# Forming the low part of a split weight by an adding transfer instead of a VectorE subtraction, for 120 of 168 weight tiles

## The chip, the cores and the metric

The kernel runs on one core of a Trainium2 chip. The metric is device time in microseconds for one execution of the whole program. The engines are named as in the profile: PE (TensorE, with PEld for its weight loads), DVE (VectorE), ACT (ScalarE), POOL (GpSimd) and SP (SyncE, which here only issues transfers).

## The reference, cut to what matters

One inference step of a decoder trunk of two layers, in float32, for 512 prompt tokens and 32 sample tokens (8 sequences of 4), which share all weights. Model width 1024, FFN width 2816, 16 query heads and 4 key heads of 64, window 128, depthwise convolution of 31 taps. Each layer is an FFN, a mixing stage, and a second FFN, with a norm behind each:

```python
x = layer_norm(ALPHA * x + 0.5 * swiglu(x, ffn1_up, ffn1_down), ...)
proj = x @ w_in + b_in
q, k, v, glu, gates = jnp.split(proj, SPLITS, axis=-1)
u = u_a * jax.nn.sigmoid(u_g)
attn = window_attention(q, k, v, ...)          # ALiBi and sinks
c = silu(layer_norm(causal_depthwise(u, ...), ...))
mix = sigmoid(g_attn) * (attn @ w_attn_out) + sigmoid(g_conv) * (c @ w_conv_out)
x = layer_norm(ALPHA * x + mix @ w_out, ...)
x = layer_norm(ALPHA * x + 0.5 * swiglu(x, ffn2_up, ffn2_down), ...)
```

## The kernel before, in words

**Products in three passes.** A float32 operand is split into a high part, rounded to the format `F32R` that PE multiplies, and a low part, the rest. A product is three matmuls: high weight by high activation (line 432), high weight by low activation (433), low weight by high activation (434). `unit` (419) does this for one piece of weights (up to 8 blocks of 128 rows, 256 columns) and one half of the tokens (`hf`): 8 x 2 x 3 = 48 matmuls, the low part being needed at the third. The tokens, 544, lie along the free dimension and are cut at 272. The values (1103) use the same three passes in lines 1115 to 1117.

**Pieces.** `plan` lists all weight pieces in the order of their use. `fetch` (254) issues a piece's loads on SP, as two tiles `raw` of 128 x 1024 from a pool of 5 buffers. `prep` (281) then calls `halves` (272) for each tile: ACT copies it into `wh`, rounding (277), DVE subtracts `wh` from it into `wl` (278). `wh` and `wl` come from the pool `pair` with 37 buffers, which also holds activations. This way goes every piece of the mixing stage, and the first four pieces of each FFN (two of the gate half, `a`, and two of the other, `u`); 84 pieces, 168 tiles. All other FFN weights go another way, `steps` (293), planned piece by piece with costs written out by hand, and aren't touched.

**When a piece is prepared.** `W` (410) prepares pieces until two are ahead of the one asked for (four at the start of an FFN); `ahead` (405) prepares the next stage's first pieces during the last products of an FFN, with ACT's copy pinned to its place in the program (`keep_in_program_order`). Apart from such pins, the order of each engine's instructions is laid out when the program is built, by a scheduler that takes what is ready first in its own timing, and of that the earliest in the program. Each engine, POOL with its transfers included, then executes its list strictly in order.

**The mixing stage** (`mix`, 984) takes its pieces in the order k, ug0, ua0, v, q0, q1, ug1, ua1, q2, q3, ug2, ua2, ug3, ua3, ga0, ga1, ao0, ga2, ao1, ga3, ao2, ao3, then four each of gc, co and wo. `ug` and `ua` make the gated input of the convolution; behind each of the four `ua` comes a part of the convolution, whose 30 taps per channel block run on DVE (1075) as background work, spread over the attention by `pump`. The sample tokens' part of the convolution is products on POOL (1090, 16 for each part), sums on DVE (1093) and bias additions on POOL (1094). `ga` is the attention's gate (`gate`, 1337), `ao` the attention's output product, `gc` and `co` the same for the convolution, `wo` the output. POOL also issues all small output transfers: values (1123, 1127), keys (1138, 1141), convolution state (1400, 1402).

**Norms.** `ln_fin` (451) has three steps, put off into the next products by a clock of PE's work: `centre` (a matmul for the mean at 463, DVE subtractions 468, ACT squares 472, DVE sums 474 and 481), `newton` (a matmul at 485, then a chain of some 14 tiny DVE operations, 507 to 521) and `scale` (a matmul at 493, DVE multiplications 497, then ACT's gain and bias, 530 or 1426, and the new split, 441 on ACT and 442 on DVE). The next stage's products of that half of the tokens need this split.

Of the kernel before, what the change touches and what calls it, by code (L numbers as in the profile page):

```python
# [11 lines left out]
F32 = mybir.dt.float32  # L12
F32R = mybir.dt.float32r
# [3 lines left out]
ALU = mybir.AluOpType  # L17
# [82 lines left out]
class Ker:  # L100
# [168 lines left out]
            raw.append(t)  # L269
        return key, kk, raw  # L270

    def halves(self, t, shape, small=False):

        new = lambda n: (self.f1(shape, F32R) if small else
                         self.pp.tile(shape, F32R, tag="pair", name=self.nm(n)))
        wh, wl = new("wh"), new("wl")
        ins = self.nc.scalar.copy(wh, t)  # L277
        self.nc.vector.tensor_tensor(wl, t, wh.bitcast(F32), op=ALU.subtract)  # L278
        return (wh, wl), ins

    def prep(self, pin=False, got=None):
        key, kk, raw = got or self.fetch()
        assert kk
        ms = []
        for t in raw:
            m, ins = self.halves(t, list(t.shape))
            if pin:
                self.tc.keep_in_program_order(ins)
            ms.append(m)
        self.ready.append((key, ms, kk))  # L290


# [1211 lines left out]
```

## Time and profile before

| | |
|---|---|
| Median of 3 runs | 2600.75 us (2594.13 to 2605.29) |
| Profiled execution | 2602.92 us, span 2600.8 us |
| Mean granted PE clock | 0.978 |
| ACT's share of the span | 46% |
| DVE's share of the span | 72% |
| DMA queues | 28.1% of 16 engines for SP's, 1.0% for POOL's |

A group's row in the profile gives the line, the engine, what is written from what, the shape and the count, then busy time and mean duration, then how long the engine idled before it and who ended that. Waits are given as total, number of times and longest. In a table of stretches, each row has the stretch, its length, busy time and count for each engine, the granted PE clock, the share of the DMA engines and GB/s. A row of a timeline is start, duration, engine, line, operation, tiles and count, with the idle time before it in brackets. Line 278 has one row with 168 instructions, since `halves` is a helper; places in the program are told by time.

### The profile page before, as it was taken

How to read it: one execution, taken by the hardware profiler on the slowest of the kernel's cores; microseconds unless marked ns; L12 is line 12 of the kernel's file. 1: busy time of each engine (PE TensorE's matmuls, PEld its weight loads, DVE VectorE, ACT ScalarE, POOL GpSimd, SP SyncE). 2: the span in 40 equal slices, each digit the busy share in tenths (PEclk: the TensorE clock that was granted, in tenths of full speed). 3: DMA queues.
4: the chain of work that ended last, by engine and by line, in shares of the span. 5: the costliest groups of instructions: out<-in, count | busy, mean ns of one | idle time of the engine just before them, and what ended most of it. 6: DMA issues, size and time to landing. Idle time of an engine off the chain costs nothing.

```text
span 2600.8 us, 47137 instructions
## 1 busy us (share of the span) xinstructions
PE 2522.6 (97%) x19846; PEld 2471.7 (95%) x19846; DVE 1882.3 (72%) x2955; ACT 1195.6 (46%) x2116; POOL 238.7 (9%) x323
## 2 busy tenths in 40 slices
PE   8999998999999999999999999999999999999997
PEld 8999998988999999999999999999899999999997
DVE  5776665997986577666667666669979766776665
ACT  4444434577426254444354444346873353444441
POOL 2000000722300000000100000026141000000000
PEclk9999998999999999999999999999999999999998
DMA  5333332231322223332503333322223222233321
GB/s 191 90 98 91 97 111 72 61 96 52 93 85 79 82 66 106 93 94 87 189 17 106 90 93 91 114 66 75 70 62 110 66 82 79 76 106 98 98 84 57
DMA packets 327139, 232.12 MB, mean 89 GB/s; under 512 B 43748, under 2 KB 324532, under 8 KB 326832
## 3 DMA queue, kind: packets, MB, share of 16 engines
q1 hardware_dynamic: 323088, 220.36, 28.1%
q0 software_dynamic: 3840, 8.76, 1.0%
q8 instruction: 155, 2.54, 0.4%
q14 instruction: 56, 0.46, 0.1%
HBM read 225.69 MB, written 9.16 MB: 90 GB/s over the span
## 4 chain that ended last, share of the span: by engine, by line
PE 84%; DVE 8%; ACT 4%; POOL 2%; issue 1%; DMA 0%; DVEq 0%; ACTq 0%; POOLq 0%
PE pa L646 17%; PE pa L434 17%; PE pa L432 17%; PE pa L433 17%; PE pb L646 12%; DVE pr L1075 3%; POOL f L1090 2%; DVE wl L278 1%; PE pa L1186 1%; PE pb L1215 1%; PE pb L1227 1%; DVE pr L442 1%; DVE pr L497 1%; PE pb L493 0%; ACT pr L1426 0%
## 5 line engine op out<-in xcount | busy, mean ns | idle before, releaser
L432 PE MATMUL pa<-pr,wh 128*128 128x272 f32 x2624 | 770.0, 295 | 24.0 <-ACT pr L441 18.5
L434 PE MATMUL pa<-pr,wl 128*128 128x272 f32 x2624 | 768.9, 294 | 6.2 <-DVE wl L278 6.2
L433 PE MATMUL pa<-pr,wh 128*128 128x272 f32 x2624 | 766.5, 293 | 5.8 <-DVE pr L442 5.8
L432 PEld LDWEIGHTS pa<-pr,wh 128*128 128x128 f32 x2624 | 502.2, 192 | 31.5 <-ACT pr L441 21.7
L433 PEld LDWEIGHTS pa<-pr,wh 128*128 128x128 f32 x2624 | 506.0, 193 | 10.6 <-DVE pr L442 8.2
L434 PEld LDWEIGHTS pa<-pr,wl 128*128 128x128 f32 x2624 | 502.8, 192 | 7.2 <-DVE wl L278 7.0
L432 PE MATMUL pa<-pr,wd 128*128 128x272 f32 (+2 forms) x1408 | 406.0, 289 | 3.2 <-ACT wd L308 3.2
L434 PE MATMUL pa<-pr,wd 128*128 128x272 f32 (+2 forms) x1408 | 408.1, 290 | 0.4 <-DVE wd L298 0.4
L433 PE MATMUL pa<-pr,wd 128*128 128x272 f32 (+2 forms) x1408 | 405.6, 288 | 0.0
L1075 DVE SCALAR_TENSOR_TENSOR pr<-u,cw,pr 128x512 f32<-128x512 f32 x480 | 349.5, 779 | 1.9 <-ACT pr L1068 1.7
L432 PEld LDWEIGHTS pa<-pr,wd 128*128 128x128 f32 x1408 | 265.5, 189 | 3.4 <-ACT wd L308 3.3
L433 PEld LDWEIGHTS pa<-pr,wd 128*128 128x128 f32 x1408 | 267.2, 190 | 0.0
L434 PEld LDWEIGHTS pa<-pr,wd 128*128 128x128 f32 x1408 | 265.5, 189 | 0.9 <-DVE wd L298 0.8
L646 PE MATMUL pa<-pr,wa 128*128 128x272 f32 x1728 | 241.4, 289 | 0.0
L646 PE MATMUL pb<-pr,ws 128*128 128x272 f32 x1728 | 239.4, 288 | 0.0
L278 DVE TENSOR_TENSOR wl<-raw,wh 128x1024 fp32r<-128x1024 f32 x168 | 204.8, 1238 | 34.4 <-ACT wh L277 33.8
L646 PEld LDWEIGHTS pa<-pr,wa 128*128 128x128 f32 x1728 | 227.1, 188 | 0.0
L646 PEld LDWEIGHTS pb<-pr,ws 128*128 128x128 f32 x1728 | 224.9, 188 | 0.0
L277 ACT CAST wh<-raw 128x1024 fp32r<-128x1024 f32 x168 | 170.9, 1047 | 93.7 <-PE pa L433 41.9
L699 DVE SCALAR_TENSOR_TENSOR pr<-pa,pr 128x544 f32<-128x544 f32 (+2 forms) x160 | 115.3, 723 | 133.0 <-PE pa L434 131.4
L664 ACT COPY pb<-pa 128x272 f32<-128x272 f32 x72 | 26.6, 370 | 295.9 <-PE pa L646 295.9
L442 DVE TENSOR_TENSOR pr<-f,pr 128x544 fp32r<-128x544 f32 x124 | 89.2, 723 | 83.1 <-ACT pr L441 83.0
(226 smaller groups left out, 3743.8 us busy)
## 6 DMA issues: line engine op xcount, KB each, us to landing
raw<-in_ffn_up_dram SPq DMA_DIRECT2D x174, 512.0 KB, 4.0
raw<-in_ffn_down_dram SPq DMA_DIRECT2D x80, 512.0 KB, 3.4
raw<-in_w_in_dram SPq DMA_DIRECT2D x72, 512.0 KB, 4.3
raw<-in_w_in_dram SPq DMA_DIRECT2D x64, 128.0 KB, 2.8
raw<-in_w_attn_out_dram SPq DMA_DIRECT2D x32, 256.0 KB, 4.0
raw<-in_w_conv_out_dram SPq DMA_DIRECT2D x16, 512.0 KB, 3.5
raw<-in_w_out_dram SPq DMA_DIRECT2D x16, 512.0 KB, 3.9
raw<-in_ffn_down_dram SPq DMA_DIRECT2D x16, 256.0 KB, 2.7
```

The costliest lines, as they stand in the source:

```text
L277: ins = self.nc.scalar.copy(wh, t)
L278: self.nc.vector.tensor_tensor(wl, t, wh.bitcast(F32), op=ALU.subtract)
L432: pin(self.nc.tensor.matmul(o, lhsT=wh, rhs=h, start=k == 0, stop=False))
L433: pin(self.nc.tensor.matmul(o, lhsT=wh, rhs=lo, start=False, stop=False))
L434: pin(self.nc.tensor.matmul(o, lhsT=wl, rhs=h, start=False, stop=k == kk - 1))
L442: pin(self.nc.vector.tensor_tensor(lo, src, hi.bitcast(F32), op=ALU.subtract))
L497: nc.vector.tensor_tensor(y[:, :, hs], y[:, :, hs], rb, op=ALU.mult)
L646: mm = lambda a, b, first=False, last=False: pin(nc.tensor.matmul(o, lhsT=a, rhs=b, start=first, stop=last, skip_group_check=True))
L664: pin(act.copy(A, b1))
L699: pin(nc.vector.scalar_tensor_tensor(Y[p][:, :, hs], ps, 0.5, Y[p][:, :, hs], op0=ALU.mult, op1=ALU.add))
L1075: self.last["cw"] = nc.vector.scalar_tensor_tensor(cc[:, m, 0:SEQ], u[:, m, k:k + SEQ], cw[:, 8 * k + c:8 * k + c + 1], cc[:, m, 0:SEQ], o ...
L1090: nc.gpsimd.tensor_tensor(pr[:, 4 * b:4 * b + 4, :], win, wv.unsqueeze(1).to_broadcast([128, DS, KC]), op=ALU.mult)
```

## The change

`halves` is told by the piece's key which of two ways to take. In the new one ACT writes `-raw`, rounded, into `wl` (the negated high part; it needs `raw` alone, not `wh`), and POOL issues a transfer from `raw` to `wl` within SBUF that adds to what lies there, so that `wl` becomes `raw` less its high part. DVE has no part in it. The new way is taken by the four first pieces of each FFN except the first layer's first, and in the mixing stage by k, v, ug0, ua0 and all of ga, ao, gc, co and wo; the four q and the other six of ug and ua, and the first FFN's, keep the subtraction. Where `prep` pins, both ACT instructions are pinned now. Nothing else differs.

```diff
-    def halves(self, t, shape, small=False):
-
-        new = lambda n: (self.f1(shape, F32R) if small else
-                         self.pp.tile(shape, F32R, tag="pair", name=self.nm(n)))
-        wh, wl = new("wh"), new("wl")
-        ins = self.nc.scalar.copy(wh, t)
-        self.nc.vector.tensor_tensor(wl, t, wh.bitcast(F32), op=ALU.subtract)
-        return (wh, wl), ins
+    def halves(self, t, shape, by_dma, pin):
+
+        wh, wl = (self.pp.tile(shape, F32R, tag="pair", name=self.nm(n)) for n in ("wh", "wl"))
+        pin(self.nc.scalar.copy(wh, t))
+        if by_dma:
+            pin(self.nc.scalar.mul(wl, t, -1.0))
+            self.nc.gpsimd.dma_start(wl.bitcast(F32), t, accum_op=ALU.add)
+        else:
+            self.nc.vector.tensor_tensor(wl, t, wh.bitcast(F32), op=ALU.subtract)
+        return wh, wl
+
+    @staticmethod
+    def by_dma(key):
+
+        l, kind = key[0], key[1]
+        if kind in ("ffn1", "ffn2"):
+            return (l, kind) != (0, "ffn1")
+        return kind in ("k", "v", "ga", "ao", "gc", "co", "wo") or key[1:] in (("ug", 0), ("ua", 0))
...
-            m, ins = self.halves(t, list(t.shape))
-            if pin:
-                self.tc.keep_in_program_order(ins)
-            ms.append(m)
+            ms.append(self.halves(t, list(t.shape), self.by_dma(key),
+                                  self.tc.keep_in_program_order if pin else lambda i: i))
```

## The prediction

> **What bounds the kernel now.** I read the page's busy times first, then who waited for whom on PE, then the stretches in which PE idles, and last the rows of each engine inside those stretches.
>
> ```profile
> span 2600.8 us, 47137 instructions
> PE 2522.6 (97%) x19846; PEld 2471.7 (95%) x19846; DVE 1882.3 (72%) x2955; ACT 1195.6 (46%) x2116; POOL 238.7 (9%) x323
> 750.00:800.00 50.00, 50.00 (x400) 49.84 (x399) 32.09 (x56) 23.71 (x37) 0.00 (x0) 1.00 0.22 68
> PE pa L434 <- DVE wl L278: 6.2, 3, 3.8
> L278 DVE TENSOR_TENSOR wl<-raw,wh x168: 1205/1222/1578, 10.4 to 2212.3; 128x1024 fp32r<-128x1024 f32 x168
> L277 ACT CAST wh<-raw x168: 1029/1048/1076, 9.3 to 2210.1; 128x1024 fp32r<-128x1024 f32 x168
> ```
>
> PE is the bound: 97% busy, and an undisturbed 50 us hold 400 matmuls, 0.125 us each. So a DVE instruction less is worth nothing by itself; what counts is the idle PE time, 78.2 us (span less busy), and the half clock behind a gap. Only 6.2 us are put down to the low parts of line 278. The others are links of the norms, which the low parts can lengthen by standing in front of them on DVE.
>
> What a gap costs with its half clock is read from stretches: matmuls missing from 8 per us, times 0.125.
>
> ```profile
> 680.00:690.00 10.00, 8.20 (x53) 7.98 (x52) 10.00 (x13) 2.47 (x4) 0.00 (x0) 0.83 0.54 161
> 1964.00:1974.00 10.00, 6.15 (x31) 5.93 (x30) 10.00 (x12) 2.88 (x4) 0.06 (x1) 0.66 0.43 121
> 811.00:824.00 13.00, 10.15 (x69) 9.94 (x68) 10.92 (x15) 10.09 (x17) 0.00 (x0) 0.87 0.26 82
> 2100.00:2110.00 10.00, 7.15 (x38) 6.93 (x37) 7.92 (x13) 8.55 (x15) 0.00 (x0) 0.66 0.32 104
> 938.00:946.00 8.00, 4.94 (x27) 4.51 (x26) 6.81 (x12) 6.94 (x13) 0.00 (x0) 0.79 0.00 1
> 1292.00:1312.00 20.00, 11.04 (x54) 9.68 (x53) 16.34 (x37) 8.51 (x16) 0.00 (x0) 0.66 0.24 73
> 401.00:417.50 16.50, 8.67 (x40) 7.51 (x39) 13.63 (x33) 8.51 (x16) 0.00 (x0) 0.59 0.00 0
> ```
>
> Columns: stretch, length, then busy time and count of PE, PEld, DVE, ACT, POOL, then granted clock. Lost: 3.4, 6.1, 4.4, 5.3, 4.6, 13.3 and 11.5 us.
>
> **The change, and what it takes away.** By the rule in the diff 120 of the 168 tiles change: 24 in three FFN starts, 48 in each mixing stage (k, v, the first ug and ua, all of ga, ao, gc, co, wo). DVE loses 120 x 1.22 = 146 us, ACT gains 120 multiplies, POOL 120 DMA issues.
>
> The gain is at the gaps. First the ao stage, where PE waits for the low part itself:
>
> ```profile
> 682.97 0.53 PE L434 MATMUL pa<-pr,wl 128*128 128x272 f32 x1 [1.80 <-DVE wl L278]
> 1968.32 0.59 PE L434 MATMUL pa<-pr,wl 128*128 128x272 f32 x1 [3.85 <-DVE wl L278]
> ```
>
> Both go, with their half clock: 3.4 + 6.1 = 9.5 us. At the norm between the layers (1292) four low parts stand among its sums on DVE; the norm at 401 has none in the same place and loses 11.5 against 13.3: gain 1.8. The convolution's norms (811 and 2100) lose 4.4 and 5.3, but the gap there ends on ACT:
>
> ```profile
> 814.67 2.62 DVE L497 TENSOR_TENSOR pr<-pr,pb 128x544 f32<-128x544 f32 x4 [0.67 <-PE pb L493]
> 818.14 0.52 PE L432 MATMUL pa<-pr,wh 128*128 128x272 f32 x2 [2.85 <-ACT pr L441]
> 802.10 0.61 PE L485 MATMUL pb<-ones,pr 128*91 128x1 f32 x6 [0.89 <-DVE pr L481]
> ```
>
> DVE itself idled 0.67 us there, for line 493 on PE, so no low part came last and the gain is not direct: PE's place for line 493 has to come earlier, because the order is laid out with less on DVE. I take half, 4.8 of 9.7; of the two gaps of 0.89 at line 485 (801 and its twin) also half, 0.9, since ACT's squares get multiplies beside them. The norm at 938 (4.6 in each layer) ends on ACT too, and ACT is nearly full there (6.94 of 8 us): I take nothing. **Gains: 17.0 us, between 9.5 and 32.**
>
> **What it adds.** A low part was ready 1.05 + 1.22 us after the cast began. Now it is a cast, a multiply, a POOL issue and a landing. The multiply is bounded below by the cast, 1.05, and above by a scaled copy of 1088 columns, 1.11; I take 1.05, same width. No accumulating transfer is in the trace. Its nearest rows:
>
> ```profile
> L573 ACT ACTIVATE pr<-pr x16: 1105/1108/1118, 51.3 to 2246.5; 128x1088 f32<-128x1088 f32 x16
> L809 POOL DMA_DIRECT2D at<-in_ln_g_dram x1 | 0.6, 565 | 580.4 <-PE pa L646 580.4
> at<-in_ln_g_dram POOLq DMA_DIRECT2D x1, 512.0 KB, 4.0
> at<-in_ln_b_dram POOLq DMA_DIRECT2D x1, 512.0 KB, 4.9
> out_new_v_prompt_dram<-at POOLq DMA_DIRECT2D x2, 128.0 KB, 2.3
> out_new_k_sample_dram<-in_cache_k_dram POOLq DMA_DIRECT2D x2, 992.0 KB, 9.5
> ```
>
> Issue 0.57, landing between 2.3 (a quarter of the bytes) and 9.5 (twice the bytes, about what reading two operands for one result moves); I take 4.5, the mean of the two rows with the same bytes from the same queue. From the start of the cast that is 1.05 + 1.05 + 0.57 + 4.5 = 7.2 us instead of 2.3, and each raw buffer is held 5 us longer; where a piece is prepared while the one before it runs (96 matmuls, 12 us) that is hidden, with 5 us to spare; without that cover it would cost what the next three places cost. The Trainium skill's "DMA: Bandwidth & Descriptors", section on the anatomy of a SWDGE DMA, puts such a transfer at about 2.0 us plus bytes over 436 GB/s; as an estimate that is 3.2 us for 512 KB, and the total below would be some 6 us less by it; the rows of 4.0 and 4.9 lie above it.
>
> Three places have no such cover. *The first ua.* Two units of 16 low-part matmuls (k, ug) precede it, so its own is the 33rd of line 434 after 410:
>
> ```profile
> 410.00:427.15 17.15, 9.90 (x32) 6.98 (x33) 0.80 0.00 1
> 427.18 0.29 PE L434 MATMUL pa<-pr,wl 128*128 128x272 f32 x1
> 423.41 2.95 ACT L277 CAST wh<-raw 128x1024 fp32r<-128x1024 f32 x3
> ```
>
> Cast from 423.41, landing at 430.6, need at 427.18: 3.4 us late. The next work, v, needs a low part too and the other half of the tokens waits for its norm, so nothing fills in. With the half clock (gaps of 1.80, 2.85 and 3.85 lost 1.6 to 2.4 us more than themselves, I take 2.0) 5.4 per layer: 10.8, between 2.4 (landing 2.3) and 23 (landing 9.5). *The second up-piece of FFN 2*:
>
> ```profile
> 914.37 1.04 ACT L277 CAST wh<-raw 128x1024 fp32r<-128x1024 f32 x1
> 912.05:920.05 8.00, 4.54 (x17) 3.04 (x17) 1.00 0.01 3
> ```
>
> The same way: the row counts line 434 from the start of the first up-piece's unit, so its 17th, just before 920.05, is the second piece's; landing at 921.5, 1.5 late; the second layer repeats it, 3.0 in all, between 0 (landing 2.3) and 17 (landing 9.5, half clock with it). ACT's squares of the norm there queue behind the multiplies; I set that against the six low parts that leave DVE. *The second ga.* This one is moved into POOL's queue, which is in order. A POOL DMA that is ready waits there behind the convolution's products:
>
> ```profile
> 473.48 0.67 POOL L1123 DMA_DIRECT2D out_new_v_prompt_dram<-at  x1
> 474.19 20.97 POOL L1094 TENSOR_SCALAR pr<-pr,vec 128x16 f32<-128x16 f32 x2
> 662.37 9.63 POOL L1090 TENSOR_TENSOR f<-f,cw 128x124 f32<-128x124 f32 x13
> 671.99 1.60 POOL L1094 TENSOR_SCALAR pr<-pr,vec 128x16 f32<-128x16 f32 x4
> 655.77 1.03 ACT L277 CAST wh<-raw 128x1024 fp32r<-128x1024 f32 x1
> 1945.66 6.36 POOL L1090 TENSOR_TENSOR f<-f,cw 128x124 f32<-128x124 f32 x13
> 668.70 0.28 PE L434 MATMUL pa<-pr,wl 128*128 128x272 f32 x1
> 1952.00 0.28 PE L434 MATMUL pa<-pr,wl 128*128 128x272 f32 x1
> ```
>
> Cast from 655.8, the second ga's DMA could be issued at 657.9, but the convolution's products are earlier in the program and all ready. Line 1090 ends at 672.0 and 1952.0; a DMA behind it lands 5.1 us later, 677.1 and 1957.1, for needs at 668.7 and 1952.0 (the first unit of the second ga, right behind the transposes of line 1396): 8.4 and 5.1 late. With fewer low parts on DVE I expect the first layer's products to run as fast as the second's (6.4 us for 13 against 9.6), so 5.1 for both, and 2.0 of half clock: 14.2 us, between 0 (the DMA passes ahead of line 1090: 663.0 at the latest) and 28 (landing 9.5). Behind the waiting DMA on POOL stand line 1094's additions and the nine small output DMAs of lines 1400 and 1402; nobody on PE waits for those.
>
> **Sum.** Losses 10.8 + 3.0 + 14.2 = 28.0, gains 17.0: +11.0 us. The profiled execution took 2602.9 (span 2600.8), the median of the runs is 2600.75; on the latter it makes **2612 us**, 0.4% slower.
>
> **Rivals.** *Faster: the transfer is quick and POOL lets it pass.* With a landing near 2.3 us and the second ga's DMA ahead of line 1090, the losses shrink to 2.4, and gains between 17 and 26 (the norms' places on PE move as well) leave about -19: 2582. It decides where that DMA is issued before 660 and the landing is under 3 us. For it: POOL is idle in most of the span (9%), and a transfer within SBUF needs no HBM. Against it: the rows of 4.0 and 4.9, and line 1123, which did not pass.
>
> *Much slower: POOL is locked out while DVE runs its taps.* Line 1094's pair took 20.97 us although four take 1.60 at 672: it started as DVE began an unbroken row of two-operand work and ended with it.
>
> ```profile
> 473.86 4.70 DVE L1075 SCALAR_TENSOR_TENSOR pr<-u,cw,pr 128x512 f32<-128x512 f32 x7
> 494.59 0.33 DVE L1196 CUSTOM_DVE_ANT_0 at<-pa,nd,nsk 128x128 f32<-128x128 f32 x1
> L1402 POOL DMA_DIRECT2D out_new_conv_sample_dram<-at x16: 497/512/516, 674.1 to 1963.5; - x16
> ```
>
> If POOL's transfers are held like that, those of ga and ao land up to 20 us late in both layers: some 15 us of stall each plus half clock instead of the second ga's 14.2, and the 9.5 of the ao stage are not won: about +40, 2641. It decides once a transfer issued beside the taps lands over 8 us later; a slow accumulation everywhere (landing 8 instead of 4.5, 3.5 more at each of the six places and half clock at all) would come to much the same, 2637. Against it: line 1402 issued beside such a row of taps (from 674) in 0.51 us each. The Trainium skill's "SBUF — State Buffer", section "Who interferes with whom", says that a DVE instruction with two SBUF inputs keeps out a GpSimd instruction that reads SBUF, and that descriptor writing is starved only by DVE's two-port modes; line 1094's 20.97 us agrees with the first half, line 1402 with the second.
>
> *Nothing to tell:* the order laid out anew puts other matmuls into the three holes and the norms stay as they are: 2602.
>
> **Chances and range.** A measurement of this kernel can tell about 0.5%, 13 us, from no change. The forecast case gets 0.45; its terms are good to some 10 us, so it is split, 0.24 within 0.5% and 0.21 beyond. The faster rival 0.25 (0.22 beyond 0.5%), the two ways to about 2640 together 0.22, nothing to tell 0.08. That makes 0.22 faster, 0.35 same, 0.43 slower. Range 2583 to 2640: it leaves out half of each outer rival. By itself the forecast case spans 2602 to 2622.
>
> **What would show it.** Right: in the waits on PE line 278 is gone from the ao stage and the accumulating DMA takes its place at the first ua (about 3 us), the second ga (about 5) and the start of FFN 2; POOL issues the second ga's DMA after its sixteenth line 1090. Wrong: a landing below 3 us or above 8, those DMAs ahead of line 1090, PE idle below 70 us, or gaps at the convolution's norm unchanged.

## The result, and the profile after

The changed kernel takes 2628.36 us (median of 6 runs, 2625.55 to 2634.74) against 2600.03 of the kernel before (6 runs): ratio 1.0113, 95% interval 1.0103 to 1.0123. That is 28 us slower. The forecast was +11 (2612), inside 2583 to 2640: the side is right, the size is two fifths of what came. Of all executions reported below one stands apart, 13833 us in the run that transfers second tiles only; that run's ratio leaves it out.

These are lines of the page of the changed kernel (line 442 is what was 434, line 278 is now the transfer):

```profile
span 2626.1 us, 47459 instructions
PE 2530.0 (96%) x19846; PEld 2477.3 (94%) x19846; DVE 1748.5 (67%) x2835; ACT 1319.0 (50%) x2244; POOL 348.4 (13%) x443
L442 PE MATMUL pa<-pr,wl 128*128 128x272 f32 x2624 | 771.0, 295 | 29.7 <-DMA wl<-raw 28.9
L278 POOL DMA_DIRECT2D wl<-raw x120 | 105.7, 932 | 1624.2 <-ACT wl L277 1513.1
wl<-raw POOLq DMA_DIRECT2D x120, 512.0 KB, 6.7
```

DVE lost 134 us of work, and PE gained 17.9 us of idleness: 96.1 us (span less busy) after 78.2. The other 7.4 us of the longer span are busy time, matmuls at half clock behind the new holes. The third line says what the holes wait for: PE stood 28.9 us waiting for transfers into wl, where before 6.2 us were put down to DVE's subtraction. Here are the longest of them, in the trace of PE (what ended the wait is in the brackets), with two other waits, at 691 and 925:

```profile
429.28 0.59 PE L442 MATMUL pa<-pr,wl 128*128 128x272 f32 x1 [3.13 <-DMA wl<-raw]
675.34 0.59 PE L442 MATMUL pa<-pr,wl 128*128 128x272 f32 x1 [5.17 <-DMA wl<-raw]
690.74 0.40 PE L440 MATMUL pa<-pr,wh 128*128 128x272 f32 x1 [0.45 <-ACT f L1360]
832.57 0.59 PE L442 MATMUL pa<-pr,wl 128*128 128x272 f32 x1 [3.54 <-DMA wl<-raw]
925.11 0.39 PE L440 MATMUL pa<-pr,wh 128*128 128x272 f32 x1 [3.51 <-ACT pr L449]
939.11 0.39 PE L442 MATMUL pa<-pr,wl 128*128 128x272 f32 x1 [2.20 <-DMA wl<-raw]
958.89 0.39 PE L442 MATMUL pa<-pr,wl 128*128 128x272 f32 x1 [1.48 <-DMA wl<-raw]
1728.13 0.39 PE L442 MATMUL pa<-pr,wl 128*128 128x272 f32 x1 [1.39 <-DMA wl<-raw]
1974.74 0.60 PE L442 MATMUL pa<-pr,wl 128*128 128x272 f32 x1 [5.17 <-DMA wl<-raw]
2130.74 0.39 PE L442 MATMUL pa<-pr,wl 128*128 128x272 f32 x1 [3.57 <-DMA wl<-raw]
2245.38 0.40 PE L442 MATMUL pa<-pr,wl 128*128 128x272 f32 x1 [1.00 <-DMA wl<-raw]
2253.00 0.39 PE L442 MATMUL pa<-pr,wl 128*128 128x272 f32 x1 [1.32 <-DMA wl<-raw]
```

429 and 1728 are the first ua, 675 and 1975 the second ga, 691 the ao stage, where the hole of 1.80 is down to 0.45 and no longer waits for a low part. 832 and 2131 are a place that the prediction didn't have: the second co piece, right behind the convolution's norm. 939, 959, 2245 and 2253 are FFN 2's start, and 925 is the norm in front of it, which waits for ACT.

**A ledger by place.** Every kernel here has the same 19846 matmuls, so the start of the n-th in one kernel can be set against the start of the n-th in the kernel before. What this shift grows by across a stretch is what that place costs, with its half clock. Both layers added, in us, each from one profiled execution (negative is a gain; the second layer's matmuls come some 9900 later, and the choice of the exact borders moves an entry by up to 0.5):

| place (matmuls of the first layer) | forecast | changed | change at FFNs only | at the mixing stage only | multiplies only | without late pieces | second tile only | without second co |
|---|---|---|---|---|---|---|---|---|
| first ua (3100-3250) | +10.8 | +9.8 | +0.6 | +7.8 | +1.1 | +0.1 | +0.9 | +9.8 |
| second ga and ao stage (5020-5250) | +4.7 | +6.1 | -5.7 | +6.9 | -6.5 | -8.0 | -5.7 | +6.8 |
| convolution's norm, second co (5900-6350) | -5.7 | +3.1 | -0.2 | +3.8 | +15.9 | -6.9 | -5.3 | -6.6 |
| FFN 2's start (6860-7250) | +3.0 | +12.8 | +17.2 | +3.4 | +4.0 | +1.7 | -4.8 | +15.1 |
| norm at 1292 (9900-10000, one place) | -1.8 | -1.9 | -2.6 | +0.1 | +0.9 | -2.7 | -2.6 | -1.6 |
| everything else | 0 | -4.8 | -2.4 | -1.9 | -0.9 | -6.8 | -2.7 | -5.8 |
| sum | +11.0 | +25.1 | +6.9 | +20.1 | +14.5 | -22.6 | -20.1 | +17.7 |

Of "everything else" 2.8 us of the changed kernel lie in the first 40 us of the program, which the change doesn't touch; there the runs differ from each other by up to 3.2, so a single profile is good to some 3 us. (The run with the FFNs only shows it most: its profiled execution took 4.7 us less than its median.)

**What the ledger doesn't show for the ao stage.** The gain there looks like the forecast's 9.5: 8.0 us without the late pieces. But the run with the FFNs only, where DVE forms every low part of the mixing stage as before, gains 5.7 at the same matmuls, and the run with the multiplies only gains 6.5. In both PE still waits there for DVE's low part; the holes of before were 1.80 and 3.85 us. The two layers of the first run, then the first layer of the second run:

```profile
681.05 0.39 PE L442 MATMUL pa<-pr,wl 128*128 128x272 f32 x1 [1.80 <-DVE wl L280]
1970.88 0.39 PE L442 MATMUL pa<-pr,wl 128*128 128x272 f32 x1 [1.83 <-DVE wl L280]
680.98 0.39 PE L442 MATMUL pa<-pr,wl 128*128 128x272 f32 x1 [1.09 <-DVE wl L278]
```

In the first of these runs the two holes shrink by 2.0 us in all, by the order laid out anew. The other 3.7 are the clock: in the 10 us around these holes it was granted at 0.83 and 0.66 before and at 1.00 in both places here, although the hole of 1.80 is the same. No more than 1.5 to 2.3 us of the gain is shown to be the work that left DVE; and what a hole costs beyond itself isn't a fixed sum, as the 2.0 of the prediction takes it to be.

### The profile page after: what moved, and what is told of

Read it like the earlier page. It is cut to its first block, busy times and chain, and to the rows that moved or that the text cites. A ratio compares the mean times of both kernels' runs of the same rounds, so it can differ in the third digit from the quotient of the medians.

```text
span 2626.1 us, 47459 instructions
## 1 busy us (share of the span) xinstructions
PE 2530.0 (96%) x19846; PEld 2477.3 (94%) x19846; DVE 1748.5 (67%) x2835; ACT 1319.0 (50%) x2244; POOL 348.4 (13%) x443
## 4 chain that ended last, share of the span: by engine, by line
PE 53%; issue 6%; DMA 2%; POOL 1%; DVE 1%; ACT 1%; DVEq 0%; POOLq 0%; SPq 0%; ACTq 0%
PE pa L654 12%; PE pa L442 9%; PE pa L440 9%; PE pa L441 9%; PE pb L654 9%; DMA wl<-raw 1%; POOL f L1098 1%; DMA raw<-in_ffn_up_dram 1%; PE pa L1194 0%; PE pb L1223 0%; PE pb L1235 0%; POOL wl L278 0%; PE pb L668 0%; DVE at L854 0%; PE pb L1125 0%
## 5 line engine op out<-in xcount | busy, mean ns | idle before, releaser
L442 PE MATMUL pa<-pr,wl 128*128 128x272 f32 x2624 | 771.0, 295 | 29.7 <-DMA wl<-raw 28.9
L1083 DVE SCALAR_TENSOR_TENSOR pr<-u,cw,pr 128x512 f32<-128x512 f32 x480 | 344.0, 772 | 2.5 <-ACT pr L1076 2.2
L278 POOL DMA_DIRECT2D wl<-raw x120 | 105.7, 932 | 1624.2 <-ACT wl L277 1513.1
```

The source lines that it names most:

```text
L278: self.nc.gpsimd.dma_start(wl.bitcast(F32), t, accum_op=ALU.add)
L442: pin(self.nc.tensor.matmul(o, lhsT=wl, rhs=h, start=False, stop=k == kk - 1))
L1083: self.last["cw"] = nc.vector.scalar_tensor_tensor(cc[:, m, 0:SEQ], u[:, m, k:k + SEQ], cw[:, 8 * k + c:8 * k + c + 1], cc[:, m, 0:SEQ], o ...
```

## The experiments

Theory A: each loss is a low part that lands after PE wants it, at a few places, and the rest of the change is a gain. Rival, theory B: ACT is late, since 120 multiplies of 1.06 us push its casts and the norms' work back, and the wait for the transfer is only where that shows. Each ratio is to executions of the kernel before taken beside that run, whose median lay between 2597.7 and 2601.5; medians of different experiments compare to some 3 us.

### The change in halves

```
@@ FFNs only
-        return kind in ("k", "v", "ga", "ao", "gc", "co", "wo") or key[1:] in (("ug", 0), ("ua", 0))
+        return False
@@ mixing stage only
-            return (l, kind) != (0, "ffn1")
+            return False
```

> Only the 24 tiles of the three FFN starts are formed by transfer, the mixing stage's 96 by DVE. Theory A (late transfers: every loss is a low part that lands after PE wants it, place by place): the losses of FFN 2's two starts stay (8.9+1.3-3.1 and 7.1+2.0-3.2, 13 us), the norm at 1292 keeps its gain of 1.9: about +11 on the kernel before, 2611 us. Theory B (ACT is what is late: its multiplies push casts and norms back, the transfer's wait is the symptom): FFN 2's casts have only its own 6 multiplies a layer in front, the mixing stage's last ones are gone, so the casts come 2 to 8 us sooner: +2 to +5, 2602 to 2605.

> Only the mixing stage's 96 tiles are formed by transfer, the FFN starts by DVE. Theory A: first ua +10.1, second ga +14.6, second co +9.9, ao stage -8.5, convolution's norms -6.9, some small ones: about +17 to +19, 2618 us. Theory B: much the same, since 80% of the multiplies stay: +20 to +24, 2622. The two runs must add up to the whole change (28) if the places do not act on each other.

FFNs only: 2614.63 us, ratio 1.0057 (1.0040 to 1.0075), +15. Mixing stage only: 2622.35, ratio 1.0080 (1.0068 to 1.0092), +21. So FFN 2's starts lose 17 us with their own transfers, with few multiplies ahead of them, and 3.4 without: against B's places, for A's, though the first run's time lies above both forecasts. The mixing stage's run tells nothing between the two. The halves make 36 against 29 for the whole, so the places do act on each other, by some 6 us.

### Multiplies without transfers

```
             pin(self.nc.scalar.mul(wl, t, -1.0))
-            self.nc.gpsimd.dma_start(wl.bitcast(F32), t, accum_op=ALU.add)
+            self.nc.vector.tensor_tensor(wl, t, wh.bitcast(F32), op=ALU.subtract)
```

> ACT does all 120 multiplies, but nothing is transferred: DVE then overwrites the tile with the difference, as before. DVE and its order are as loaded as before, ACT as loaded as in the changed kernel. Theory A: none of the waits on the transfer, the ao stage's waits on DVE as before: 2598 to 2606. Theory B: the casts and norms on ACT are as late as in the changed kernel, so most of the +28 stays: 2615 to 2630.

2617.97 us, ratio 1.0062 (1.0050 to 1.0074): A's number is missed and B's is met, but not at B's places. First ua, second ga and FFN 2, where the changed kernel loses 28.7, cost -1.4 here; 15.9 lie at the convolution's norms, where the changed kernel's own norm gains. This is what happens there. A norm ends in fourteen small steps on DVE (lines 515 to 529; 507 to 521 before), each of which needs the one before. First and last of them in the kernel before, in the changed kernel and in this one:

```profile
802.75 0.16 DVE L507 TENSOR_SCALAR nw<-pb 91x3 f32<-91x3 f32 x1 [0.80 <-PE pb L485]
810.38 0.15 DVE L521 TENSOR_TENSOR nw<-nw,nw 91x3 f32<-91x3 f32 x1
```

```profile
800.43 0.16 DVE L515 TENSOR_SCALAR nw<-pb 91x3 f32<-91x3 f32 x1 [0.80 <-PE pb L493]
802.91 0.16 DVE L529 TENSOR_TENSOR nw<-nw,nw 91x3 f32<-91x3 f32 x1
```

```profile
802.33 0.15 DVE L515 TENSOR_SCALAR nw<-pb 91x3 f32<-91x3 f32 x1
808.60 1.21 DVE L278 TENSOR_TENSOR wl<-raw,wh 128x1024 fp32r<-128x1024 f32 x1
811.07 1.21 DVE L278 TENSOR_TENSOR wl<-raw,wh 128x1024 fp32r<-128x1024 f32 x1
812.84 0.15 DVE L529 TENSOR_TENSOR nw<-nw,nw 91x3 f32<-91x3 f32 x1
822.52 0.59 PE L440 MATMUL pa<-pr,wh 128*128 128x272 f32 x1 [8.51 <-ACT pr L449]
```

7.8 us before, 2.6 after, 10.7 with the multiplies but without the transfers: other work of DVE gets between the steps, here two subtractions among it, and PE then stands still for 8.5 us. In the kernel before no low part stands between them, only other work (lines 442 and 567). But every run that takes subtractions off DVE in this stage has the steps together and gains here, but for late second co pieces; the two that take none off there (FFNs only, multiplies only) have them spread and don't. So the change's gain at the norm is real and comes with less work on DVE; a multiply on ACT isn't free, but with DVE relieved its cost doesn't show at this place. (Here a subtraction also waits for its multiply, at the head of DVE's queue. How much of the 15.9 that is, stays open.)

### Without the pieces that came late

```
+        late = (("ua", 0), ("ga", 1), ("co", 1), ("ffn2", "u", 0), ("ffn2", "a", 1), ("ffn2", "u", 1))
+        if key[1:] in late:
+            return False
```

> The whole change without the pieces that came late: first ua, second ga, second co and the last three of FFN 2's start are formed by DVE again, 24 tiles; 96 stay with the transfer. Theory A: the change's +28 less 10.1 + 14.6 + 9.9 + 13: -19 to -20 on the kernel before, 2580 us. Theory B: 80% of the multiplies stay and so does most of the loss: 2615 to 2622.

2582.66 us, ratio 0.9926 (0.9914 to 0.9939): 46 us off the changed kernel for 24 tiles of 120, where A said 48 and B said 6 to 13. On PE 0.3 us of waiting for a transfer are left:

```profile
PE pa L445 <- DMA wl<-raw: 0.3, 1, 0.3
```

Theory B falls as the cause of the change's loss: 96 multiplies are still there, and the 24 that went with the late pieces cost little at the first ua, the second ga and FFN 2 in the run before.

### What makes a transfer late: the adding

```
-            self.nc.gpsimd.dma_start(wl.bitcast(F32), t, accum_op=ALU.add)
+            self.nc.gpsimd.dma_start(wl.bitcast(F32), t)
```

> The whole change, but the 120 transfers copy the raw weights over the negated high part instead of adding them to it: the subtraction is left out, the bytes, the queue and all waits stay. Theory A1 (the adding makes the transfers slow, so that they back up when issued every 1.9 us: alone 4.4 us, the fourth and fifth in a row 10 to 11): a copy lands in under 4 us also in a row, FFN 2's starts lose 5 us less each, the whole 2612 to 2618. Theory A2 (any 512 KB in this queue takes as long): landings of 4.4 alone and 8 to 11 in a row as before, 2623 to 2633.

2607.11 us, ratio 1.0034 (1.0021 to 1.0048): 21 us less than the changed kernel, more than A1 said. In the changed kernel the five transfers of FFN 2's start follow each other every 1.9 us, as fast as ACT casts and multiplies; first their issues on POOL, then how long each took to land, in the same order, then the stretch:

```profile
933.11 0.87 POOL L278 DMA_DIRECT2D wl<-raw  x1 [39.02 <-ACT wl L277]
935.00 0.87 POOL L278 DMA_DIRECT2D wl<-raw  x1 [1.02 <-ACT wl L277]
936.90 0.87 POOL L278 DMA_DIRECT2D wl<-raw  x1 [1.03 <-DVE nw L517]
939.03 0.87 POOL L278 DMA_DIRECT2D wl<-raw  x1 [1.26 <-ACT wl L277]
940.69 0.87 POOL L278 DMA_DIRECT2D wl<-raw  x1 [0.79 <-ACT wl L277]
```

```profile
DMA to landing us min/median/max: 6.0/6.0/6.0
DMA to landing us min/median/max: 6.5/6.5/6.5
DMA to landing us min/median/max: 8.1/8.1/8.1
DMA to landing us min/median/max: 9.9/9.9/9.9
DMA to landing us min/median/max: 11.3/11.3/11.3
931.00:950.00 19.00, 16.80 (x116) 16.58 (x115) 7.49 (x23) 14.00 (x16) 4.74 (x6) 0.85 0.86 174
```

The same stretch with plain copies, and each kernel's queue and landings, the changed one first:

```profile
920.00:940.00 20.00, 18.25 (x126) 17.71 (x126) 11.20 (x30) 18.00 (x24) 2.81 (x6) 0.84 0.56 197
```

```profile
q0 software_dynamic: 21120, 71.68, 13.7%
DMA to landing us min/median/max: 4.4/6.7/13.4
```

```profile
q0 software_dynamic: 21120, 71.68, 7.5%
DMA to landing us min/median/max: 2.8/3.7/8.9
```

The last two columns of a stretch are the busy share of the 16 DMA engines and what they moved: 0.86 for 174 GB/s with adding, 0.56 for 197 without. Out of the queue's share, less the 1.0% that it had before: 12.7% of 2626 us for 120 transfers are 2.78 us of all 16 engines for one addition, and 6.5% of 2608 are 1.41 for a copy of the same bytes in the same number of packets. With 2.78 of work every 1.9 us, and the weights' loads beside it, the engines fill up and each transfer lands later than the one before it. They land 2.5, 3.4, 4.0 and 3.0 us after each other. The quickest addition lands in 4.4 us and the quickest copy in 2.8; below, "alone" means these.

The Trainium skill's "DMA: Bandwidth & Descriptors", section on the anatomy of a SWDGE DMA, gives 3.2 us by the estimate in the prediction; the copy alone (2.8) is 0.4 below it, the addition 1.2 above it alone (4.4) and 3.5 in the middle (6.7).

### What makes the second ga late: its place in POOL's queue

```
+                    if p == 3:
+                        while self.loaded < self.pi + 2:
+                            self.prep()
                     conv()
```

> The whole change, but the second ga is prepared ahead of the last convolution's products in the program, so that POOL issues its transfers before line 1098's sixteen products and not behind them. Theory A (the transfer stood behind them in POOL's queue): the two gaps of 5.17 us at the second ga go, with their half clock, 14.6 in all: 2614 us, and the landing is at 664 or earlier. Theory C (transfers beside DVE's taps are held up): they are issued early but land at 670 or later, and the gaps stay: 2626 to 2630.

2617.92 us, ratio 1.0073 (1.0060 to 1.0086): 10.4 us less than the changed kernel, and in the ledger the ga and ao stages go from +6.1 to -7.4, 13.5 of the forecast 14.6. POOL in the changed kernel, then here:

```profile
659.97 10.89 POOL L1098 TENSOR_TENSOR f<-f,cw 128x124 f32<-128x124 f32 x13
670.80 1.77 POOL L278 DMA_DIRECT2D wl<-raw  x2
```

```profile
655.03 0.86 POOL L278 DMA_DIRECT2D wl<-raw  x1 [5.91 <-ACT wl L277]
656.93 0.84 POOL L278 DMA_DIRECT2D wl<-raw  x1 [0.83 <-ACT wl L277]
660.24 12.39 POOL L1101 TENSOR_TENSOR f<-f,cw 128x124 f32<-128x124 f32 x16
```

The transfers stood behind the last thirteen products, as forecast; put ahead of them they are issued 14 to 16 us sooner and land after 5.9 and 6.5 us, by 663.4, beside DVE's taps. Theory C falls: nothing holds them there for longer than 6.5 us, and their issues take 0.86 and 0.84. That is also what the Trainium skill's "SBUF — State Buffer", section "Who interferes with whom", says of descriptor writing beside such work of DVE.

### The second co alone

```
+        if key[1:] == ("co", 1):
+            return False
```

> The whole change with one piece undone, the second co (2 tiles a layer). Theory A (the norm's hole on PE was really closed, and only this low part, cast 6.8 us ahead of its need, opens another): its gaps of 3.54 and 3.57 us shrink to under 1, 10 us with their half clock: 2618 us. Theory D (the hole only moves: something else of the norm, on ACT or DVE, is late in its place): under 3 us, 2625 to 2630.

2619.11 us, ratio 1.0086 (1.0072 to 1.0099): 9.3 us less by the medians and 7 by the ratios, for four tiles, with 9.7 at its place in the ledger; A said 10. The hole doesn't reappear elsewhere at the norm (0.61 us are left in each layer, for DVE's low part of the same piece). What had happened is read from ACT, first before, then after:

```profile
808.50 1.04 ACT L277 CAST wh<-raw 128x1024 fp32r<-128x1024 f32 x1
```

```profile
821.76 4.12 ACT L574 ACTIVATE pr<-pr 128x1088 f32<-128x1088 f32 x4
825.78 1.04 ACT L275 CAST wh<-raw 128x1024 fp32r<-128x1024 f32 x1
826.72 1.07 ACT L277 ACTIVATE wl<-raw 128x1024 fp32r<-128x1024 f32 x1
828.08 0.87 POOL L278 DMA_DIRECT2D wl<-raw  x1 [24.90 <-PE pa L442]
```

Before, this piece was cast at 808.5 and wanted at 826.0, 17.5 us later. In the changed kernel ACT comes to it only after the norm's scaled copies of line 574, at 825.78, and PE, whose holes at the norm are gone, wants it at 829.0. A landing 4.4 us after the issue at 828.08 is 832.5, when PE starts. With the cast and a subtraction of 1.22 it would have been there at 828.0.

### Other ways to cut it, and the best version

```
-            ms.append(self.halves(t, list(t.shape), self.by_dma(key),
+            ms.append(self.halves(t, list(t.shape), i == 1 and self.by_dma(key),
```

> Only the second tile of each of the 60 pieces is formed by transfer, the first by DVE: half the transfers and multiplies, no more than one in 3.8 us, and a tile that PE wants 3 us later. Theory A: first ua 1.6 late instead of 3.1, second ga 3.6 instead of 5.2, second co and FFN 2's pieces in time: losses of about 15 instead of 48, and half of the gains of 17 to 23: 2602 to 2608 us. Theory B (ACT): half the multiplies, half the loss: 2614.

2582.83 us, ratio 0.9941 (0.9928 to 0.9954): 20 us better than I expected. Half the tiles bring most of the gain at the norms and the ao stage, and at FFN 2's start more than the whole change without its late pieces; the norm's hole of 3.51 us on ACT, which both the changed kernel and the run without the late pieces have in front of FFN 2, doesn't open in this run. Why not wasn't followed further. Little comes late, as the second tile of a piece is wanted 3 us after the first and transfers follow each other at half the rate. What is left is mostly the second ga behind POOL's products, with holes of 1.90 and 1.84 us.

In the run without the late pieces, the negation was moved from ACT to DVE:

```
-            pin(self.nc.scalar.mul(wl, t, -1.0))
+            self.nc.vector.tensor_scalar_mul(wl, wh.bitcast(F32), -1.0)
```

> The run without the late pieces (2582.7 us), but the negated high part of the 96 tiles is made by DVE and not by ACT. Theory A (what that run gains is the relief of DVE at the norms and the ao stage): DVE has a pass of its own again, so most of the gain is lost: 2592 to 2602. Theory B (ACT's multiplies are what still costs there, DVE's relief is worth little): faster, 2570 to 2578.

```profile
L277 DVE TENSOR_SCALAR wl<-wh x96: 680/694/831, 375.6 to 2163.0; 128x1024 fp32r<-128x1024 f32 x96
```

2602.30 us, ratio 1.0017 (1.0007 to 1.0027): 96 passes of 0.69 us on DVE, 67 us in all, take the whole gain of 19 away again, as A said. But not where A said. Counted as in the ledger, the convolution's norms keep their gain (-6.6), with the fourteen steps as close together as in the changed kernel, from 798.75 to 801.27. The loss against the run without the late pieces lies at the ga and ao stages (12.7), the first ua (6.1) and FFN 2's start (3.1). At the ao stage transfers are late again, 4.2 us in each layer:

```profile
688.02 0.57 PE L445 MATMUL pa<-pr,wl 128*128 128x272 f32 x1 [4.24 <-DMA wl<-raw]
```

There the cast of ACT is done by 674.3, but DVE gets to the negation only at 682.45, behind taps and splits, and POOL issues the transfer at 683.43. So ACT's multiplies are the cheaper place, because there they don't make the transfers late; that all of the 19 us were DVE's relief this run doesn't show.

Last, two combinations: the second tile only, without the second ga; and the late mixing pieces on DVE with second tiles only at FFN 2 and wo.

```
@@ first combination
+        if key[1:] == ("ga", 1):
+            return False
@@ second combination
+        if key[1:] in (("ua", 0), ("ga", 1), ("co", 1)) or (kind in ("ffn2", "wo") and i == 0):
+            return False
```

> The run with only the second tile by transfer (2582.8 us), and the second ga on DVE altogether. Theory A (what still waits at the ga stage is that one tile behind POOL's products, gaps of 1.90 and 1.84 us): both gaps go, with their half clock 1.5 to 3.5 each, 2576 to 2580. If DVE is late there without the relief: no change, 2583.

> The best of both, place by place: first ua, second ga and second co on DVE, of FFN 2's start and wo only the second tile by transfer, all else of the change by transfer. Theory A (places do not act on each other, so the better of the two ledgers can be taken at each): the 22.7 that the run without the late pieces gained, and 4.5 + 2.0 more at FFN 2's starts: -29, 2571 us, between 2568 and 2576. Theory B' (the stages act on each other through the order): no better than 2580.

2577.93 us, ratio 0.9930 (0.9918 to 0.9943), and 2577.83, ratio 0.9928 (0.9915 to 0.9940). The first is as expected: the two holes at the second ga are gone. The second missed its 2571: each place came as its ledger said but FFN 2's start (-3.4 where -4.8 was taken over), and "everything else" gave 3.5 instead of 6.8. Both are 0.7% under the kernel before; by their intervals they can't be told from the run without the late pieces.

## Why the prediction was wrong, point by point

**Right.** What bounds the kernel. The gains: 1.8 forecast at the norm at 1292, 1.9 measured, and nothing (0.1) with the mixing stage only; 4.8 + 0.9 at the convolution's norms, 6.6 measured (without the second co). The "half" taken there was a guess that came out by luck; what the traces show there is that the norm's fourteen steps are no longer interleaved with other work.

**Right in size, not in cause.** 9.5 forecast at the ao stage, 8.0 measured where nothing covers it (without the late pieces). The prediction put it all down to the low parts that leave DVE; 5.7 and 6.5 came in runs where DVE kept them.

**Right.** The first ua: 10.8 forecast, 9.8 measured, though not with the forecast's 3.4 us of lateness in both layers (3.13 and 1.39); its transfer landed after 6.2 us in the first layer and 4.4 in the second, and why the first took longer stays open. The second ga: 14.2 forecast, holes of 5.17 twice, 14.6 in the ledger up to matmul 5100 and 15000, and the mechanism, POOL's queue, shown by undoing it. The landing of one transfer by itself: 4.5 taken, 4.4 measured; the multiply 1.05, measured 1.06. The issue is longer than taken (0.87 for 0.57), but lies within the landing's time, which counts from its start: the chain alone is 6.7 us, not 7.2.

**Wrong: "the second up-piece of FFN 2", 3.0.** Measured 12.8 for FFN 2's start. The step priced only the first of six tiles, with the landing of a lone transfer, and let ACT's queue be set off against DVE's. That first tile came near the forecast: holes of 2.20 and 0.20 us, some 4.5 with their half clock. The rest was left out. Five of the six come some 1.9 us apart, an addition keeps the 16 engines busy for 2.78, and the third lands after 8.1, the fifth after 11.3 us. PE waits for the fourth in the second layer (landed after 9.9) and for the sixth in both (9.2 and 8.8; on ACT its cast in the first layer had also waited 4.97 us for its load). The norm itself, set to nothing here, costs some 3 of the 12.8; the run with the mixing stage only has 3.4 at this place without a transfer or a multiply of FFN 2, so the multiplies of these tiles aren't what does it. The transfers were priced by latency, and nobody asked for how long one occupies the engines. The range had 17 for "landing 9.5"; that end was the nearer one. Of the 12.8, 11 go when the three late pieces are on DVE.

**Wrong: "where a piece is prepared while the one before it runs that is hidden, with 5 us to spare".** For the second co it wasn't: 9.7 by the ledger, 7 to 9 by the clock. The slack was read from the order of before, and the change lays the order out anew: ACT came to this cast later among the norm's work, and the gain at the norm made PE come to it sooner. The one gain was spent on this.

**The sum.** By the ledger the named places came to 9.8 + 14.6 - 8.5 - 6.6 + 9.7 + 12.8 - 1.9 = 29.9 us (first ua, second ga, ao stage, convolution's norms, second co, FFN 2's starts, norm at 1292) where the forecast had 11.0. Of the 18.9 between them 19.5 are the two failed steps; the others differ from their forecasts by 1 us or less each. The rest of the program was 4.8 faster in the profile, which makes 25.1; the medians differ by 28.3.

Two of the prediction's side sums are off and change nothing: the upper end for the first ua is 2 x (3.4 + 5.0 + 2.0) = 20.8 and not 23, and a landing of 3.2 us in place of 4.5 would make the total 7.8 us less (1.3 at each of six places), not some 6.

**The rivals.** The faster one needed a landing near 2.3 us and the second ga ahead of POOL's products: neither was so. POOL locked out beside the taps was not so either. The other half of the slow rival, "a slow accumulation everywhere (landing 8 instead of 4.5)", was nearest to the truth: 6.7 in the middle, but by a full row of DMA engines, and not everywhere.

## What to carry to other kernels

Price a transfer that stands in for an engine's work twice: how long until it lands, and for how long it occupies the DMA engines; if the engine that feeds it makes one faster than that, each lands later than the last. Hand over to it only pieces whose cover is longer than the whole chain (here cast, multiply and landing, 6.7 us alone and 13.6 for the fifth in a row), and check that cover in the order after the change, since the gain itself moves the place where the piece is wanted. Where the work moved is relief and not a bound, try half of it: here 60 tiles gained about as much as the best 96.

## What the runs showed of the hardware

An adding transfer within SBUF keeps the 16 DMA engines busy for 2.78 us per 512 KB, a plain one for 1.41; its issue holds POOL for 0.87 us, a plain one's for 0.53; the quickest landed in 4.4 us, plain in 2.8. One addition with no other near it, but beside 1.06 MB of the weights' loads (issued at 372.48), landed after 8.9 us. What a hole on PE costs beyond itself differs: behind the same hole of 1.80 us the clock granted over 10 us was 0.83 in one program and 1.00 in another.

The loads of the attention output's weights, issued in the stretch where the ga and ao pieces are transferred, became late as well, in the changed kernel:

```profile
raw<-in_w_attn_out_dram SPq DMA_DIRECT2D x32, 256.0 KB, 7.5
```

It was 4.0 us in the kernel before and with the FFNs' transfers only, 7.7 with the mixing stage's, 5.2 with half of all transfers, and 6.8 with plain copies: here the adding matters less than that there are transfers at all. No wait on PE was traced to it.
